# The RWKV-7 recurrence inside a deep fp32 block stack: each step taken straight from the state instead of from a map formed per chunk and head

## The chip, the cores and the metric

One Trainium2 chip, one core of it. The metric is the device time of one execution in microseconds; lower is better. The program is built ahead of time: for each engine (TensorE, VectorE, ScalarE, GpSimd, and SyncE, which starts the DMA transfers) the order of its instructions is fixed when it is built, each engine takes its own list in that order, and an instruction that has to wait holds back everything behind it on that engine. In the profile the engines are called PE, DVE, ACT, POOL and SP.

## The reference

A stack of transformer-like blocks in fp32 on 512 tokens: projections, several kinds of attention, gated feed-forward layers. The part that matters is one mixer (the "even" one) whose second half of the heads is an RWKV-7 recurrence: 8 heads of width 64, a 64x64 state S for each head, run once forwards and once backwards over the tokens. First the context tokens are scanned, then the latent ones start from the context's last state:

```python
def step(S, inp):
    r, w, k, v, kk, a = inp
    S = (S * w[:, :, None, :]
         - jnp.einsum('bhvk,bhk->bhv', S, kk)[..., None] * (kk * a)[:, :, None, :]
         + v[..., None] * k[:, :, None, :])
    return S, jnp.einsum('bhvk,bhk->bhv', S, r)
...
S_cf, y_cf = wkv7_scan(S0, dir_inputs(f_ctx, 0), reverse=False)
S_cb, y_cb = wkv7_scan(S0, dir_inputs(f_ctx, 1), reverse=True)
_, y_lf = wkv7_scan(S_cf, dir_inputs(f_lat, 0), reverse=False)
_, y_lb = wkv7_scan(S_cb, dir_inputs(f_lat, 1), reverse=True)
o_lat = rwkv7_readout(y_lf + y_lb, f_lat, r_k, gn_w, gn_b)
```

Each token decays the state (w), removes what the state holds along kk, adds the product of v and k, and reads the state with r. The other half of that mixer's heads is ordinary attention, which does not depend on the recurrence.

## The kernel before, in words

The scan is done in chunks of 64 tokens. The 512 tokens are four tiles of 128 tokens, two chunks each; a tile in one direction is a *unit*, so there are eight units, and eight *steps*, each of which takes one chunk in the forward direction and one in the backward direction (d = 0, 1) further. Both directions share every instruction: the forward chunk lies on one half of the 128 partitions, the backward chunk on the other.

For each unit, before its steps:

- *front* and *back* (`rwkv_in`) make the decayed vectors. `ar` holds, per head pair, the decay on a diagonal, the read vectors and the removal vectors; `g` holds, per head and chunk, what the chunk's tokens add to the state (columns 0 to 63), the token-by-token products that outputs read (64 to 127) and those that the removal reads (128 to 191).
- Within a chunk the removals depend on one another through a unit lower triangular 64x64 matrix per head and chunk, which has to be inverted. *solve* (`rwkv_solve`) inverts its 16x16 diagonal pieces for two units at once by 28 small DVE operations on two tiles `dl` and `dt`, loaded by a DMA from a DRAM buffer `dq` and stored by a DMA to a DRAM buffer `dy`.
- `rwkv_maps` loads those pieces as `x` (L1603), and extends them to the whole inverse by two rounds of `product` and `update` (all four go through `each`, L1609). Then it forms, per chunk and head, the chunk's *map*: `am` holds the removal vectors transposed (L1635) and the values times the removal products (the third kind of product at L1609, `m<-lw,g`); the inverse is applied to it (L1649); the result is copied into `lw`, beside the values `v` that were loaded there (L1588); and `lw` times `g` (L1663), plus `ar`, is written over `g` as `z`.

`z` is one matrix per chunk and head which, multiplied with the state, gives the next state and the chunk's outputs. For that the state tiles `si` hold, beside each head's 64x64 state on one half of the partitions, an identity on the other half, written once at the start; the values pass through it. Two `si` tiles alternate.

`rwkv_step` then is two groups of 16 matmuls: the next state (L1681), copied out of PSUM by DVE for the even heads and ACT for the odd ones into the other `si` tile, and the outputs (L1690), written to `yac` by ACT for the first direction that reaches a tile and added to `yac` by DVE for the second.

What sets the order: `rwkv` runs four *blocks* p = 1 to 4. In each, `maps_of(p-1)` makes the maps of two units and takes two steps; after every `yield` of it one piece of the independent attention is issued (`fill`), then two pieces of `ahead_of(p)`, which prepares the next two units (back, solve, front), and two pieces of the gates and readouts of finished tiles. `ahead_of` has nothing left in the fourth block. The scheduler that builds the program takes the instructions in about this order and interleaves them on each engine by what is ready. After the fourth block comes `mixed`, the projection back to the residual, which needs the outputs of all steps; its weight loads start behind the last step.

PSUM has two buffers with the name `m` here, which all the products share, and one `y`, used by the steps.

## Time and profile before

| what | time |
|---|---|
| median of 3 runs | 2336.53 us |
| lowest and highest of them | 2333.61 and 2338.04 us |
| the profiled execution, its own time | 2338.83 us |
| the span of the profiled execution | 2337.0 us |

The span is the time from the first to the last instruction of the profiled execution; the views below all belong to that one execution. PE is busy for 2250.4 us of it. The recurrence, with the attention woven into it, lies between about 929 and 1173 us from the start of the span. A matmul in fp32 appears as two records in the trace, each with a time of its own; "busy" for PE counts the union of overlapping records, while the mean ns of a group is the length of one record, overlaps and all. The granted clock (PEclk) is a share of the full 2.4 GHz: 1.00 is that level all the time, 0.50 is 1.2 GHz all the time.

### The profile page before, as it was taken

The numbers are of one execution on the slowest core, as the hardware profiler recorded it, in microseconds if no ns is written. First come the engines' busy times: TensorE is split into PE (matmuls) and PEld (weight loads), VectorE is DVE, ScalarE is ACT, GpSimd is POOL, SyncE is SP. The second block draws the span as 40 slices with busy tenths as digits, with TensorE's granted clock in tenths as the row PEclk, the third lists the DMA queues.
The fourth block names the chain that finished last, engine by engine and source line by source line (L and its number), as shares of the span: only waits on it lengthen the run. The fifth ranks groups of instructions, "written<-read, shape, count | busy, mean of one in ns | idle before, by whom it ended". The sixth has DMA issues, their size and how long they took to land.

```text
span 2337.0 us, 35487 instructions
## 1 busy us (share of the span) xinstructions
PE 2250.4 (96%) x13714; PEld 1841.1 (79%) x13714; DVE 1563.4 (67%) x2993; ACT 1074.5 (46%) x1887; POOL 5.6 (0%) x10
## 2 busy tenths in 40 slices
PE   8999999999999998998889999999999999999998
PEld 6688788877787786776667778787778788768998
DVE  7867778766845768878588677437755334787555
ACT  6756666322224638765535222224422223476444
POOL 0000000000000000000000000000000000000000
PEclk9999999999999999999989999999999999999999
DMA  8556544554623535332354455323553222314553
GB/s 294 175 185 207 179 149 163 191 179 159 202 96 110 172 139 146 102 91 69 85 203 145 166 189 176 131 89 121 179 189 125 92 98 92 104 37 142 185 183 119
DMA packets 161944, 342.01 MB, mean 146 GB/s; under 512 B 48624, under 2 KB 76272, under 8 KB 161648
## 3 DMA queue, kind: packets, MB, share of 16 engines
q1 hardware_dynamic: 161056, 339.15, 43.8%
q8 instruction: 108, 1.77, 0.3%
q10 hardware_dynamic: 720, 0.60, 0.1%
q14 instruction: 60, 0.49, 0.1%
HBM read 321.86 MB, written 17.84 MB: 145 GB/s over the span
## 4 chain that ended last, share of the span: by engine, by line
PE 88%; DVE 6%; ACT 4%; DMA 2%; issue 1%; SPq 0%; DVEq 0%; ACTq 0%
PE mm L113 25%; PE mm L115 24%; PE mm L114 24%; PE m L1609 1%; PE tr L217 1%; PE m L1663 1%; DVE wlo L96 1%; PE po L1047 1%; PE wm L272 1%; PE wm L329 1%; PE gg L1540 1%; PE tr L1047 1%; ACT whi L95 1%; PE po L531 1%; PE y L1681 1%
## 5 line engine op out<-in xcount | busy, mean ns | idle before, releaser
L95 ACT CAST whi<-raw 128x1024 fp32r<-128x1024 f32 (+2 forms) x437 | 437.3, 1001 | 956.9 <-PE mm L114 587.4
L113 PE MATMUL mm<-xh,whi 128*128 128x512 f32 (+1 forms) x1912 | 679.8, 359 | 12.8 <-ACT xh L95 5.7
L115 PE MATMUL mm<-xh,wlo 128*128 128x512 f32 (+1 forms) x1912 | 679.2, 356 | 4.7 <-DVE wlo L96 4.3
L114 PE MATMUL mm<-xl,whi 128*128 128x512 f32 (+1 forms) x1912 | 679.1, 356 | 1.2 <-DVE xl L96 1.1
L96 DVE TENSOR_TENSOR wlo<-raw,whi 128x1024 fp32r<-128x1024 f32 (+2 forms) x437 | 507.9, 1164 | 249.5 <-ACT whi L95 243.1
L113 PEld LDWEIGHTS mm<-xh,whi 128*128 128x128 f32 x1912 | 363.4, 191 | 77.1 <-ACT whi L95 17.4
L115 PEld LDWEIGHTS mm<-xh,wlo 128*128 128x128 f32 x1912 | 363.9, 191 | 58.2 <-DVE wlo L96 8.4
L114 PEld LDWEIGHTS mm<-xl,whi 128*128 128x128 f32 x1912 | 364.3, 191 | 55.2 <-DVE xl L96 3.9
L115 PE MATMUL mm<-hh,wlo 128*128 128x512 f32 (+1 forms) x704 | 260.3, 370 | 0.0
L114 PE MATMUL mm<-hl,whi 128*128 128x512 f32 (+1 forms) x704 | 258.4, 367 | 0.1
L113 PE MATMUL mm<-hh,whi 128*128 128x512 f32 (+1 forms) x704 | 257.0, 366 | 0.0
L127 DVE SCALAR_TENSOR_TENSOR macc<-raw,modc,macc 128x1024 f32<-128x1024 f32 x189 | 234.9, 1280 | 0.8 <-DMA raw<-in_w_mod 0.3
L127 DVE SCALAR_TENSOR_TENSOR xres<-mm,mod,xres 128x256 f32<-128x256 f32 x216 | 96.6, 480 | 161.8 <-PE mm L115 161.4
L118 DVE TENSOR_TENSOR fg<-mm,fg 128x512 f32<-128x512 f32 (+1 forms) x84 | 52.4, 624 | 162.2 <-PE mm L115 162.1
L113 PEld LDWEIGHTS mm<-hh,whi 128*128 128x128 f32 x704 | 132.2, 188 | 27.6 <-ACT whi L95 2.5
L114 PEld LDWEIGHTS mm<-hl,whi 128*128 128x128 f32 x704 | 132.2, 188 | 26.1 <-DVE hl L96 0.7
L113 PE MATMUL mm<-whi,xh 128*128 128x512 f32 (+1 forms) x360 | 143.6, 404 | 8.9 <-ACT whi L95 8.4
L115 PEld LDWEIGHTS mm<-hh,wlo 128*128 128x128 f32 x704 | 132.5, 188 | 22.8
L114 PE MATMUL mm<-wlo,xh 128*128 128x512 f32 (+1 forms) x360 | 143.5, 399 | 2.8 <-DVE wlo L96 2.8
L115 PE MATMUL mm<-whi,xl 128*128 128x512 f32 (+1 forms) x360 | 141.9, 396 | 0.0
L113 PEld LDWEIGHTS mm<-whi,xh 128*128 128x128 f32 x360 | 68.7, 191 | 30.0 <-issue 9.2
L114 PEld LDWEIGHTS mm<-wlo,xh 128*128 128x128 f32 x360 | 69.0, 192 | 17.1 <-DVE wlo L96 5.2
(401 smaller groups left out, 2539.6 us busy)
## 6 DMA issues: line engine op xcount, KB each, us to landing
raw<-in_ffn_in SPq DMA_DIRECT2D x176, 512.0 KB, 3.5
raw<-in_w_mod SPq DMA_DIRECT2D x144, 512.0 KB, 4.5
raw<-in_ffn_out SPq DMA_DIRECT2D x64, 448.0 KB, 3.2
raw<-in_w_in_even SPq DMA_DIRECT2D x32, 512.0 KB, 4.9
raw<-in_w_in_odd SPq DMA_DIRECT2D x32, 512.0 KB, 4.1
raw<-in_ffn_out SPq DMA_DIRECT2D x32, 512.0 KB, 3.6
raw<-in_w_ple_gate SPq DMA_DIRECT2D x16, 512.0 KB, 3.7
raw<-in_even_r SPq DMA_DIRECT2D x15, 512.0 KB, 3.6
```

The source lines that it names most:

```text
L95: S.copy(out=hi, in_=src)
L96: V.tensor_tensor(out=lo, in0=src, in1=r32(hi), op=ALU.subtract)
L113: E.matmul(out=ps, lhsT=ah, rhs=bh, start=first, stop=False)
L114: E.matmul(out=ps, lhsT=ah, rhs=bl, start=False, stop=False)
L115: E.matmul(out=ps, lhsT=al, rhs=bh, start=False, stop=last)
L118: V.tensor_tensor(out=o, in0=a, in1=b, op=op)
L127: V.scalar_tensor_tensor(out=o, in0=a, scalar=s, in1=b, op0=op0, op1=op1)
L217: E.transpose(ps[:, j * 128:(j + 1) * 128], s, ident)
L272: E.matmul(out=ps[32 * j:32 * j + 32, hf * 256:hf * 256 + 256], lhsT=cz[:, 4 * g + j, 10 - 2 * c:42 - 2 * c], rhs=raw[:, j], start=c == 0 ...
L329: E.matmul(out=ps[32 * j:32 * j + 32], lhsT=mod_1[:, 2 - q:34 - q], rhs=acc[:, v, hf * 512:hf * 512 + 512], start=q == 0, stop=q == 2)
L531: E.matmul(out=po[:, 0:128], lhsT=pt[:, j * 128:(j + 1) * 128], rhs=vt[:, j, c], start=j == 0, stop=j == nk - 1)
L1047: E.matmul(out=po[half(a), 0:256], lhsT=vt[:, j], rhs=pt[:, j, 2 * a:2 * a + 2], start=j == 0, stop=j == nk - 1)
```

## The change

No map is formed. `rwkv_maps` becomes `rwkv_inverse`: the inverse is built as before, the values are loaded into a tile `uv` of their own (four buffers), and the product of the values with the removal products, which went to `am`, goes to a new tile `kv`. The transposes of the removal vectors, the application of the inverse to `am`, the tiles `lw`, and the 16 matmuls, 4 additions and 4 copies per unit that made `z` are gone. The state tiles no longer hold an identity.

Each step then has four stages instead of two. The removal vectors times the state (8 matmuls, L1640) are added to `kv` by DVE; the inverse is applied to the sum (16 matmuls, L1646), and the result is copied into the free halves of `uv` by DVE for one direction and by ACT for the other; the next state (L1657) sums, in PSUM, decay times state and `g` times `uv` (32 matmuls); the outputs (L1665) sum read vectors times state and `g` times `uv` (32 matmuls), in a PSUM buffer `m` instead of `y`. There is a `yield` after the addition and after the copies into `uv`, so a step has three slots instead of one, and a unit's inverse has five instead of seven: a block has 11 slots instead of 9. The last step makes no next state.

```diff
-            eye2 = C["eye2"]
-            C["lw"] = []
-            for n in range(2):
-                C["lw"].append([pk.tile([128, 4, 4, 64], F32, tag=f"lw{n}{ch}", name=nm("lw")) for ch in range(2)])
...
-                for par in range(2):
-                    hb = half(1 - par)
-                    for d in range(2):
-                        acopy(x[hb, d, par], eye2[hb].unsqueeze(1).to_broadcast([64, 4, 64]))
...
-                    for n in (0, 1) if p % 2 == 0 else (2, 3):
-                        yield from rwkv_step(n, tiles, z, si, yac)
+                def steps(p, kv):
+                    us = sorted(order[2 * p:2 * p + 2], key=lambda un: un["d"])
+                    for s in range(2):
+                        n = 2 * (p % 2) + s
+                        yield from rwkv_step(C, us, s, kv[s], si[n % 2], si[1 - n % 2] if p < 3 or s == 0 else None, yac, n < 2)
...
-    def rwkv_maps(C, D, un):
...
+    def rwkv_inverse(C, D, un, kv):
...
+        uv = un["uv"] = wk.tile([128, 2, 8, 64], F32, tag="uv", name=nm("uv"), bufs=4)
         for ch in range(2):
-            nc.sync.dma_start(out=lw[ch][half(1 - ch), :, 1:3],
-                              in_=D["v"][half(ch), t].rearrange("p (f a v) -> p f a v", f=4, a=2))
+            nc.sync.dma_start(out=uv[half(1 - ch), ch], in_=D["v"][half(ch), t].rearrange("p (h v) -> p h v", h=8))
...
         T = product(1)
-        am = w512("am", (128, 4, 4, 64))
...
+        ps = pst("m")
+        each(ps, lambda ch, h: g[half(1 - ch), h, ch, 128:192], lambda ch, h: uv[half(1 - ch), ch, h])
+        for ch in range(2):
+            acopy(kv[ch ^ d][half(ch)], v8(ps[half(ch)]))
+        yield
+        update(T)
+        un["x1"] = x1
+        yield
...
+    def rwkv_step(C, us, s, kv, s0, s1, yac, new):
+        at = [(d, un, s ^ d, half(s ^ d), slice(64 * (s ^ d), 64 * (s ^ d) + 64)) for d, un in enumerate(us)]
         ps = pst("m")
         for f in range(4):
+            for d, un, ch, cb, cc in at:
+                E.matmul(out=ps[cb, f * 128:(f + 1) * 128], lhsT=un["ar"][:, f, 2, cc], rhs=s0[:, d, :, f], start=True, stop=True)
+        tt(kv, kv, ps.rearrange("p (h t) -> p h t", h=8), ALU.add)
+        yield
         ps = pst("m")
+        for h in range(8):
+            for d, un, ch, cb, cc in at:
+                E.matmul(out=ps[cb, h * 64:(h + 1) * 64], lhsT=un["x1"][cb, h], rhs=kv[cb, h], start=True, stop=True)
+        for (d, un, ch, cb, cc), cp in zip(at, (vcopy, acopy)):
+            cp(un["uv"][cb, ch], ps[cb].rearrange("p (h t) -> p h t", h=8))
         yield
...
+        if s1 is not None:
+            ps = pst("y")
+            for d, un, ch, cb, cc in at:
                 for f in range(4):
+                    for i in range(2):
+                        for par in range(2):
+                            lh, rh = ((un["ar"][:, f, 0, cc], s0[:, d, par, f]), (un["g"][:, 2 * f + par, ch, 0:64], un["uv"][:, ch, 2 * f + par]))[i]
+                            E.matmul(out=ps[half(par), d * 256 + f * 64:d * 256 + f * 64 + 64], lhsT=lh, rhs=rh, start=i == 0, stop=i == 1)
+            for par, cp in ((0, vcopy), (1, acopy)):
+                cp(s1[half(par), :, par].rearrange("p d f v -> p d (f v)"), ps[half(par)].rearrange("p (d x) -> p d x", d=2))
+        ps = pst("m")
+        for h in range(8):
+            for i in range(2):
+                for d, un, ch, cb, cc in at:
+                    lh, rh = ((un["ar"][:, h // 2, 1, cc], s0[:, d, h % 2, h // 2]), (un["g"][:, h, ch, 64:128], un["uv"][:, ch, h]))[i]
+                    E.matmul(out=ps[cb, h * 64:(h + 1) * 64], lhsT=lh, rhs=rh, start=i == 0, stop=i == 1)
+        for d, un, ch, cb, cc in at:
+            y = yac[cb, un["t"] % 2]
+            if new:
+                acopy(y, ps[cb])
             else:
+                tt(y, y, ps[cb], ALU.add)
         yield
```

Outside the recurrence the order of the instructions on each engine stays as it was. Three places inside it follow, all of the second block. In these rows the numbers behind a name tell its buffers apart.

On PE before, at the first of the block's two steps: the end of the maps (L1663) and the next state (L1681), with attention (L1019, L1001) and the next unit's back stage (L1540) between them.

```order
L1019 MATMUL tr_10621<-ident_63,gp_10564 128x128 x2
L1663 MATMUL m_10488<-g_9377,lw_9086 128x128 x4
L1663 MATMUL m_10495<-g_9377,lw_9086 128x128 x4
L1681 MATMUL y_10525<-si_9089,g_9377 64x64
L1001 MATMUL sc_10840<-K_10830,qS_10832 128x512 x2
L1681 MATMUL y_10525<-si_9089,g_9377 64x64 x7
L1540 MATMUL gg_10662<-ar_10648,ak_10052 128x128
L1540 MATMUL gh_10663<-ar_10648,ak_10052 128x128
```

On PE after, from the removal of that step to its next state, in two pieces (the rows between are more of L1646 and the same attention).

```order
L1640 MATMUL m_10415<-si_9081,ar_9157 64x128
L1640 MATMUL m_10415<-si_9081,ar_9352 64x128
L1001 MATMUL sc_10425<-K_9122,qS_9892 128x256 x2
L1019 MATMUL tr_10433<-ident_63,gp_10369 128x128 x2
L1388 MATMUL fr_10761<-ro_9095,ro_9096 128x512
L1646 MATMUL m_10437<-kv_9917,x_2092_9923 64x64
L1646 MATMUL m_10437<-kv_9917,x_2095_9931 64x64
L1665 MATMUL m_10503<-si_9081,ar_9157 64x64
L1001 MATMUL sc_10456<-K_9122,qS_9892 128x256 x2
L1665 MATMUL m_10503<-si_9081,ar_9352 64x64
L1388 MATMUL fr_11129<-ro_9095,ro_9096 128x512
L1657 MATMUL y_10468<-uv_9919,g_9170 64x64 x2
```

The step's stages L1640, L1646, the first matmuls of L1665 (which need only the state) and L1657 now stand apart, with attention (L1001, L1019) and the gates' matmul (L1388) between them.

On DVE before, in the same block: the next units' solve (`dt`, `dl`) alternates with the additions that made the maps (`g<-m,ar`) and with the next unit's back stage (`ak`).

```order
L118 TENSOR_TENSOR ak_10052<-ak_10052,fe_10644 128x4x128
L118 TENSOR_TENSOR dt_10288<-dl_10270 128x54
L118 TENSOR_TENSOR g_9182<-m_10446,ar_9169 64x4x128
L118 TENSOR_TENSOR dl_10270<-dl_10270,dt_10288 128x6x9
L1005 RECIPROCAL s_10504<-s_10502 128x1
L118 TENSOR_TENSOR ak_10052<-ak_10052,fe_10644 128x4x2x64
L118 TENSOR_TENSOR dt_10291<-dl_10270 128x56
L118 TENSOR_TENSOR g_9182<-m_10453,ar_9169 64x4x128
L118 TENSOR_TENSOR dl_10270<-dl_10270,dt_10291 128x7x8
```

On DVE after, at the corresponding part of the solve.

```order
L118 TENSOR_TENSOR dl_10273<-dl_10273,dt_10294 128x7x8
L118 TENSOR_TENSOR yac<-yac,m_10503 64x512
L118 TENSOR_TENSOR dt_10297<-dl_10273 128x56
L118 TENSOR_TENSOR yac<-yac,m_10503 64x512
L118 TENSOR_TENSOR dl_10273<-dl_10273,dt_10297 128x8x7
L224 COPY gpt_10360<-tr_10539 128x2x128
L118 TENSOR_TENSOR dt_10300<-dl_10273 128x54
L118 TENSOR_TENSOR kv_9918<-kv_9918,m_10543 128x512
L118 TENSOR_TENSOR dl_10273<-dl_10273,dt_10300 128x9x6
```

The solve now alternates with the steps' own DVE work: additions into `yac` and `kv`, and an attention copy (`gpt`).

On SP before, around the store of that solve's result (`dy`): loads of `v` into `lw` (L1588) stand ahead of it.

```order
L1433 DMA oTd<-go_10443 128x2x128
L1389 DMA ro_9112<-lod 128x128 x2
L1588 DMA lw_9081<-vd 64x4x128
L1588 DMA lw_9082<-vd 64x4x128
L1588 DMA lw_9085<-vd 64x4x128
L1445 DMA K_10830<-kd 128x1024
L1447 DMA qS_10834<-qd 128x512
L1588 DMA lw_9086<-vd 64x4x128
L1582 DMA dy_7266<-dl_10270 64x16x16
L1582 DMA dy_7267<-dl_10270 64x16x16
```

On SP after, around the same store and the load of its result (`x`).

```order
L1500 DMA fe_10727<-fd 128x12x128
L1437 DMA K_10580<-kd 128x1024
L1439 DMA qS_10584<-qd 128x512
L1381 DMA ro_9096<-lod 128x128 x2
L1425 DMA oTd<-go_10558 128x2x128
L1574 DMA dy_7266<-dl_10273 64x16x16
L1574 DMA dy_7267<-dl_10273 64x16x16
L1596 DMA x_2213_10701<-dy_7266 64x8x64 x2
L1582 DMA uv_11520<-vd 64x512 x2
```

The loads into `lw` are gone; the load of `v`, now into `uv`, stands behind the load of `x`.

## Rows read from the trace of the kernel before

**Rows 1.** Page parts 1 and 4: busy us, share; chain by line.

```profile
PE 2250.4 (96%) x13714; PEld 1841.1 (79%) x13714; DVE 1563.4 (67%) x2993; ACT 1074.5 (46%) x1887; POOL 5.6 (0%) x10
...
PE mm L113 25%; PE mm L115 24%; PE mm L114 24%; PE m L1609 1%; PE tr L217 1%; PE m L1663 1%; DVE wlo L96 1%; PE po L1047 1%; PE wm L272 1%; PE wm L329 1%; PE gg L1540 1%; PE tr L1047 1%; ACT whi L95 1%; PE po L531 1%; PE y L1681 1%
```

**Rows 2.** Windows, four blocks, last steps: length, busy us, PEclk.

```profile
929.00:1000.50 71.50, 64.25 (x771) 50.21 (x771) 56.54 (x132) 52.27 (x128) 5.39 (x6) 0.91 0.45 115
...
1000.50:1062.00 61.50, 58.10 (x777) 46.84 (x778) 44.65 (x103) 38.48 (x95) 0.00 (x0) 0.92 0.32 83
...
1062.00:1126.50 64.50, 55.11 (x742) 43.36 (x737) 55.21 (x130) 35.04 (x63) 0.00 (x0) 0.97 0.35 92
...
1126.50:1173.00 46.50, 39.87 (x631) 32.77 (x630) 24.03 (x48) 22.30 (x48) 0.00 (x0) 0.91 0.20 54
...
1143.90:1174.20 30.30, 23.29 (x284) 19.52 (x280) 15.02 (x27) 15.97 (x32) 0.00 (x0) 0.83 0.12 33
```

**Rows 3.** PE groups, 929 to 1173: busy us, mean ns, idle before.

```profile
L1663 PE MATMUL m<-g,lw 128*128 128x128 f32 x256 | 35.4, 284 | 2.3 <-ACT lw L221 1.1 <-ACT g L221 1.1
...
L1609 PE MATMUL m<-x,g 64*64 64x64 f32 x512 | 21.6, 232 | 2.8 <-DVE s L124 2.1 <-ACT am L221 0.7
...
L1609 PE MATMUL m<-x,T 64*64 64x64 f32 x512 | 20.8, 223 | 0.3 <-DVE T L118 0.3
...
L1649 PE MATMUL m<-am,x 64*64 64x128 f32 x256 | 17.5, 275 | 1.4 <-ACT lw L221 1.1
...
L1681 PE MATMUL y<-si,g 128*64 128x64 f32 x256 | 14.8, 248 | 4.2 <-ACT g L221 1.7 <-DVE yac L118 1.6 <-ACT yac L221 0.6
...
L1690 PE MATMUL y<-si,g 128*64 128x64 f32 x256 | 11.5, 258 | 5.5 <-ACT si L221 5.5
...
L1609 PE MATMUL m<-lw,g 64*64 64x64 f32 x256 | 9.9, 222 | 1.1 <-ACT am L221 0.9 <-issue 0.2
...
L1635 PE MATMUL m<-ident,ar 128*128 128x128 f32 x32 | 5.2, 287 | 0.0
```

**Rows 4.** Waits, 929 to 1173: us, times, longest.

```profile
PEld m L1609 <- issue: 6.3, 20, 2.2
```

**Rows 5.** Timeline, PE, second block: start us, us, what.

```profile
1061.11 1.15 PE L1690 MATMUL y<-si,g 128*64 128x64 f32 x32 [0.81 <-ACT si L221]
```

**Rows 6.** DVE and ACT groups, 929 to 1173.

```profile
L118 DVE TENSOR_TENSOR g<-m,ar 64x512 f32<-64x512 f32 x32 | 22.0, 687 | 6.6 <-PE m L1663 5.7
...
L221 ACT COPY lw<-m 64x512 f32<-64x512 f32 x32 | 18.5, 579 | 3.0 <-PE m L1649 2.6
...
L221 ACT COPY g<-m 64x512 f32<-64x512 f32 x32 | 18.5, 578 | 9.1 <-DVE g L118 8.4
```

**Rows 7.** Timeline, last two steps: start us, us, what [idle before].

```profile
1162.62 0.68 DVE L224 COPY si<-y 64x512 f32<-64x512 f32 x1 [1.93 <-PE y L1681]
...
1163.33 0.58 ACT L221 COPY si<-y 64x512 f32<-64x512 f32 x1 [1.48 <-DVE si L224]
...
1163.96 1.83 PE L1690 MATMUL y<-si,g 128*64 128x64 f32 x32 [1.38 <-ACT si L221]
...
1167.37 1.98 PE L1681 MATMUL y<-si,g 128*64 128x64 f32 x32 [1.58 <-DVE yac L118]
...
1170.74 1.97 PE L1690 MATMUL y<-si,g 128*64 128x64 f32 x32 [1.39 <-ACT si L221]
...
1172.75 0.33 SPq L100 DMA_DIRECT2D raw<-in_even_out  x1
```

**Rows 8.** SP queue: waits 929 to 1173; timeline of one load.

```profile
SPq L1588 <- PE m L1663: 26.3, 8, 8.9
...
1057.72 1.25 SPq L1603 DMA_DIRECT2D x<-dy  x2
```

**Rows 9.** Timeline, DVE, second block: solve, first and last.

```profile
1032.50 0.17 DVE L118 TENSOR_TENSOR dt<-dl 128x14 f32<-128x14 f32 x1
...
1048.08 0.18 DVE L118 TENSOR_TENSOR dl<-dl,dt 128x14 f32<-128x14 f32 x1
```

More of the change, by code (lines that the diff above doesn't have):

```diff
@@ L1289, in rwkv @@
                 side = iter(())
-                def steps(p):
-                    tiles = ((2, 3), (0, 1))[p // 2]
-                    z = {(un["d"], un["t"]): un["z"] for un in order[4 * (p // 2):2 * p + 2]}
-                    for n in (0, 1) if p % 2 == 0 else (2, 3):
-                        yield from rwkv_step(n, tiles, z, si, yac)
+                def steps(p, kv):
[3 more added lines that the diff above has]
+                        yield from rwkv_step(C, us, s, kv[s], si[n % 2], si[1 - n % 2] if p < 3 or s == 0 else None, yac, n < 2)
                 def ahead_of(p):
@@ L1308, in maps_of @@
                 def maps_of(p):
-                    for _ in itertools.zip_longest(*(rwkv_maps(C, D, order[u]) for u in (2 * p, 2 * p + 1))):
+                    kv = [C["wk"].tile([128, 8, 64], F32, tag=f"kv{i}", name=nm("kv")) for i in range(2)]
+                    for _ in itertools.zip_longest(*(rwkv_inverse(C, D, order[u], kv) for u in (2 * p, 2 * p + 1))):
                         yield
@@ L1314, in maps_of @@
                         yield from read
-                    yield from steps(p)
+                    yield from steps(p, kv)
                 for p in range(1, 5):
@@ L1639, in rwkv_maps @@
-        acopy(am[:, :, 1:3], ps.rearrange("p (f a t) -> p f a t", f=4, a=2))
-        yield
-        update(T)
-        yield
-        for i in range(2):
-            ps = pst("m")
-            for j in range(4):
-                h = 4 * i + j
-                for ch in range(2):
-                    cb = half(ch)
-                    E.matmul(out=ps[cb, j * 128:(j + 1) * 128], lhsT=x1[cb, h], rhs=am[cb, h // 2, 2 * (h % 2):2 * (h % 2) + 2],
-                             start=True, stop=True)
-            for ch in range(2):
-                acopy(lw[ch][half(ch), 2 * i:2 * i + 2], ps[half(ch)].rearrange("p (f a t) -> p f a t", f=2, a=4))
@@ L1654, in rwkv_maps @@
-        yield
-        z = g.rearrange("p (f a) c t -> p c a f t", a=2)[:, :, :, :, 0:128]
-        for ch in range(2):
-            for par in range(2):
-                ps = pst("m")
-                pz = ps.rearrange("p (f t) -> p f t", f=4)
-                hb, vb = half(par), half(1 - par)
-                for f in range(4):
-                    h = 2 * f + par
-                    E.matmul(out=ps[:, f * 128:(f + 1) * 128], lhsT=lw[ch].rearrange("p f a t -> p f (a t)")[:, f, par * 128:(par + 1) * 128],
-                             rhs=g[:, h, ch, 0:128], start=True, stop=True)
-                tt(z[hb, ch, par].rearrange("p f (a t) -> p f a t", a=2), pz[hb].rearrange("p f (a t) -> p f a t", a=2),
-                   ar[hb, :, 0:2, ch * 64:ch * 64 + 64], ALU.add)
-                acopy(z[vb, ch, par], pz[vb])
@@ L1668, in rwkv_maps @@
-        un["z"] = z
-        yield
-    def rwkv_step(n, tiles, z, si, yac):
-        s0, s1 = si[n % 2], si[1 - n % 2]
-        where = []
-        for d in range(2):
-            c = n if d == 0 else 3 - n
-            where.append((d, tiles[c // 2], c % 2))
-        ps = pst("y")
-        for d, t, ch in where:
-            for f in range(4):
-                for par in range(2):
-                    E.matmul(out=ps[half(par), d * 256 + f * 64:d * 256 + f * 64 + 64], lhsT=z[d, t][:, ch, par, f, 0:64],
-                             rhs=s0[:, d, par, f], start=True, stop=True)
-        for par, cp in ((0, vcopy), (1, acopy)):
-            cp(s1[half(par), :, par].rearrange("p d f v -> p d (f v)"), ps[half(par)].rearrange("p (d x) -> p d x", d=2))
-        ps = pst("y")
-        for f in range(4):
-            for par in range(2):
-                for d, t, ch in where:
-                    h = 2 * f + par
-                    E.matmul(out=ps[half(ch), h * 64:(h + 1) * 64], lhsT=z[d, t][:, ch, par, f, 64:128], rhs=s0[:, d, par, f], start=True, stop=True)
-        for d, t, ch in where:
-            cb = half(ch)
-            if n < 2:
-                acopy(yac[cb, t % 2], ps[cb])
```

10 lines of the change are left out of this document (2 added, 8 removed).

## The prediction

> **What bounds the kernel now.** I read the page first. PE is busy for 96% of the span, and the chain that ended last is mostly matmuls of the projections (L113 to L115); the lines of the recurrence have about 1% of it each [rows 1]. So the whole kernel is bound by PE, and whatever shortens PE's list where nothing else is late shortens the span; but the change touches one stage, and that has to be read by itself. The windows come second: 929 to 1173 us, cut at the end of each block's last step [rows 2]. PE is busy for 64.25, 58.10, 55.11 and 39.87 us of 71.5, 61.5, 64.5 and 46.5, which is 217.3 of 244 us; DVE for 180.4, ACT for 148.1 (the sums of those four rows). The stage is PE's, with 26.7 us in which PE idles; no other engine is near it, though over a few us DVE can be. The third view, PE's groups in the stage, says what that work is and where it idles [rows 3]: the two costliest groups are L1663, which forms the maps (35.4 us), and the products L1609, which stay.
>
> The last 30 us are of another kind: PE is busy for 23.3 of 30.3 us, at a granted clock of 0.83, and no attention is left to fill it [rows 2]. The timeline there shows a bare chain [rows 7]: DVE copies half of the state (0.68), ACT the other half only after it (0.58), and each of the last two output groups has waited 1.4 us for ACT. The first weight load of the projection that follows (`raw<-in_even_out`) is issued at 1172.75, some 0.04 us after the last output group ends (1170.74 + 1.97). There a microsecond of the steps is a microsecond of the span.
>
> **The change part by part: PE.** Gone are the map products 35.4, the application of the inverse 17.5, the steps' two groups 14.8 and 11.5, and the transposes 5.2 [rows 3]: 84.4 us. Added are, in records (two for each fp32 matmul), over eight steps:
>
> - Removal times state, 8 matmuls of 128 columns a step: 128 records. The nearest row is L1649, also 128 columns: 17.5 / 256 = 68 ns each. 8.7 us.
> - The inverse, 16 of 64x64 a step: 256 records. The three L1609 groups are the same shape: (21.6 + 20.8 + 9.9) / 1280 = 41 ns. 10.5 us.
> - Next state, 32 a step for seven steps (the last has none), and outputs, 32 a step for eight: 448 + 512 = 960 records of 64 columns. At best they stream as the group at 1061.11 does, 1.15 us for 32 or 36 ns [rows 5]; the two groups that they replace took (14.8 + 11.5) / 512 = 51 ns on average, the half-rate stretches included. I take 42, nearer to the streaming row, since the new groups are twice as long and wait as a whole: 40.3 us, with 34.5 and 49 as ends.
>
> That is 59.5 us (53.7 to 68.2). PE's work goes down by **25 us** (16 to 31). Nothing in it is off the path except what only fills an idle gap; in the first three blocks PE's list has attention behind each group, so what goes out moves that attention forward.
>
> **Waits.** The idle time of PE just before the removed groups and before the product from `lw` is 2.3 + 1.4 + 1.1 + 4.2 + 5.5 = 14.5 us [rows 3]; these go. New are three hand-overs a step: the addition to `kv` on DVE (0.69 by the `g<-m,ar` addition, [rows 6]), the copies into `uv` (0.68 on DVE and 0.58 on ACT, one after the other as the `si` copies are, so 1.3; [rows 7]), and the same 1.3 for the next state. In the last block nothing covers the first two: 2 x (0.7 + 1.3) = 4.0, and 0.6 for semaphores. The third is covered by the step's own outputs (64 records, 2.3 us at 36 ns) before the next step's removal. In the other six steps the order puts attention between the stages; I take 1.2 us a step there, the size of one uncovered copy, 7 in all. New waits 11.6, net **-3**. If attention covers all of them only the last block's 4.6 stay, net -10; if nothing does, 8 x 3.3 = 26.4 come, net +12.
>
> **The other engines.** DVE loses the 32 additions (22.0 us), ACT 32 copies into `lw` and 32 into `g` (18.5 each) and the copies of `am`; what comes (eight additions and eight copies on DVE at 0.69, eight copies and sixteen of `kv` on ACT at 0.58) is about 11 and 14 us [rows 6]. Off the path, so no term, except that ACT's copies into `g` had stood 8.4 us behind DVE's additions. The eight identity copies and four memsets at the start lie in a stretch with ACT at 52 of 71 us [rows 2] and are costed at nothing. On SP, the loads of `v` into `lw` had waited 26.3 us for L1663, eight times [rows 8], and held the loads behind them; those waits go. The solve is 28 small DVE operations between 1032.50 and 1048.08 [rows 9], held up by being interleaved with additions; its result is loaded at 1057.72 [rows 8], 9.6 us after it was done.
>
> **Sum.** -25 - 3 = -28 us on the profiled execution, 2338.8 to 2310.8. That execution was 2.3 us over the median, so against the median 2336.5 - 28 = **2308.5 us**. As a check from the other side, the last block: its 30.3 us hold 14 us or so of removed work and waits and get back two steps of the new kind. Two steps at full rate are (16 + 32 + 128) x 2 records less the 64 of the missing next state, 288 records at 40 ns or 11.5 us, plus 4.6 of waits, 16 to 17; at the lower clock (1.9 against 1.15 us for the same 32 records, [rows 5, 7]) some 22. The block gives 8 to 13 us, and the other three have to give 5 to 7 each.
>
> One thing in the trace speaks against this. PE's weight loads at L1609 had 20 waits that no event explains, 6.3 us in all, 0.32 each, the longest 2.2 [rows 4], where 64x64 work begins. The Trainium skill has a rule for it, in "TensorEngine Tiling (Array Packing)", section Key Properties: a change of the tiling mode drains TensorE. The trace agrees in kind; no row isolates it. A step now goes into and out of 128x64, 64x64 and again 128x64 tiles with 128x128 attention between, six changes against about four before; two more for eight steps at 0.32 us are an estimated 5 us, so by that rule the sum would be -23, without it -28.
>
> **Rivals.**
>
> *Only the last block gains.* Blocks 1 to 3 are held by the preparation of the next units: load, decay products, solve, store, load. For it: solve and load take from 1032.50 to 1057.72 [rows 8, 9], most of the second block's latter half. Against it: PE is busy for 58.1 of the 61.5 us there [rows 2], so that chain was covered. The last block gives its 11, the rest nothing: 2325.5.
>
> *More than the work.* With SP's queue free, the load of the solve's result comes up to 8.9 us earlier [rows 8], and PE, which ran at 0.92 of the clock there [rows 2], has less at the lower level (0.08 x 61.5 is some 5 us of clock, of which I count 3). -28 - 9 - 3 = -40: 2296.5. Against it stands the same 58.1 of 61.5.
>
> *The lower clock takes it back.* Steps with waits between small groups are where PE is at 1.2 GHz: 1.83 to 1.97 us for what takes 1.15 [rows 5, 7]. At that ratio, 1.65, two thirds of the 59.5 us of new work at the lower level cost 26 us more: -28 + 26, no change, 2334.5. For it: 0.83 in the last window. Against it: 0.91 to 0.97 where there is attention.
>
> *Slower.* Each of the three hand-overs waits not for its 0.7 us operation but for DVE's list: the solve's 28 operations and the attention's now stand between the `kv`, `uv` and `si` operations in blocks 1 to 3, and PE, which takes its list in order, cannot go past a waiting stage. If a step idles 7 us (2.3 at each hand-over), eight cost 56: 56 - 14.5 - 25 = +16, 2352.5. It decides from about 5 us a step (39.5 / 8). For it: the solve's 15.6 us for 28 operations of 0.17 to 0.18 [rows 9] show how crowded that list is; against it: DVE is busy for 73% of the second block [rows 2] and loses 22 us of additions.
>
> **How the numbers follow.** My forecast 0.53 (its own range 2296 to 2323: -41 from the lower ends of work and waits, down to -14 with either at its bad end); only the last block 0.16; more than the work 0.16; the lower clock 0.06; slower 0.09. Under 0.2%, some 4.7 us, a measurement of this kernel cannot tell from no change. The first three are faster, 0.85; the fourth is the same, 0.06; the last slower, 0.09. The range 2292 to 2330 takes in the first three with the bounds of their terms and leaves out the other two and a little at the low end.
>
> **What would show it.** PE's busy time in the stage: 192 us against 217 if the sum of the work is right; L1657 and L1665 together 34 to 49 us. PE's idle time before L1646, L1657 and L1640: 12 us in all, half of it in the last two steps; 40 or more would mean the slower rival, and it would name DVE's `kv` or `uv` as the releaser. From the block's last attention to the issue of `raw<-in_even_out`: 16 to 22 us where it was 30.3. If blocks 1 to 3 keep 71.5, 61.5 and 64.5 us while PE idles more, it is the first rival. If the load of `x` comes within 2 us of the solve's end and the second block is shorter by more than 10 us, it is the second. The forecast is wrong if the new small groups run near 1.65 times their streaming time in all blocks, or if PE's list, with less in it, only waits longer for the same loads.

## The result, and the profile of the kernel after

The median went from 2337.28 us (2333.61 to 2340.43, four runs) to **2307.52 us** (2305.60 to 2315.90, four runs); the ratio is 0.988, its 95% interval 0.9855 to 0.9904. That is 29.8 us between the medians, where 28 had been forecast (2308.5 us, 2292 to 2330).

The profiled execution took 2308.39 us, with a span of 2306.6. The page, parts 1 and 4:

```profile
PE 2226.5 (97%) x14002; PEld 1820.1 (79%) x14002; DVE 1550.7 (67%) x2976; ACT 1038.9 (45%) x1822; POOL 2.0 (0%) x6
...
PE mm L113 25%; PE mm L115 25%; PE mm L114 25%; PE m L1602 2%; PE tr L217 1%; PE wm L272 1%; PE po L1047 1%; PE wm L329 1%; DVE wlo L96 1%; PE gg L1532 1%; PE m L1665 1%; PE tr L1047 1%; PE po L531 1%; ACT whi L95 0%; DMA x<-dy 0%
```

The chain is the projections' as before [rows 1]. PE is busy for 23.9 us less, though it has 288 more records. The stage still begins at 929 us and now ends, with the first `raw<-in_even_out`, at 1141.49 instead of 1172.75: 31.3 us earlier, so the whole gain is in it. Its four blocks, each cut within 0.3 us of the end of its last output group, and the stage (length, busy us of PE, PEld, DVE, ACT, POOL, granted clock, DMA):

```profile
929.00:990.90 61.90, 58.80 (x875) 46.28 (x876) 49.88 (x122) 36.59 (x90) 1.84 (x2) 0.89 0.47 124
990.90:1041.90 51.00, 48.78 (x834) 38.36 (x833) 41.92 (x101) 30.60 (x81) 0.00 (x0) 1.00 0.42 99
1041.90:1105.20 63.30, 54.94 (x851) 42.44 (x851) 56.48 (x136) 32.62 (x72) 0.00 (x0) 0.95 0.35 89
1105.20:1141.49 36.29, 29.20 (x642) 24.44 (x642) 20.01 (x39) 13.15 (x29) 0.00 (x0) 0.95 0.35 96
929.00:1141.49 212.49, 191.71 (x3198) 151.52 (x3198) 168.29 (x396) 112.95 (x270) 1.84 (x2) 0.94 0.40 103
```

The stage of the kernel before, cut in the same way at its load:

```profile
929.00:1172.75 243.75, 217.33 (x2910) 173.18 (x2910) 180.19 (x411) 148.10 (x333) 5.39 (x6) 0.93 0.34 89
```

PE's busy time falls by 25.6 us and its idle time by 5.6 (26.4 to 20.8). The cuts of [rows 2] were rounded: the kernel before ended its blocks' last output groups at 1003.3, 1062.3, 1123.2 and 1172.7, so the blocks went from 74.3, 59.0, 61.0 and 49.5 us to 61.9, 51.0, 63.3 and 36.3. The third got longer: with eleven slots instead of nine the attention moves forward, the third block holds more of it and the last block less. PE's time for it (L1001, L1019, L1047) goes from 11.7 to 17.2 us in the third block and from 14.0 to 7.0 in the last, so 7 of the 13.2 us by which the last block got shorter are work that moved.

The four new groups, one row each in the order L1640, L1646, L1657, L1665 (PE and weight loads busy, over the stage):

```profile
929.00:1141.49 212.49, 8.70 (x128) 6.82 (x128) 0.94 0.40 103
...
929.00:1141.49 212.49, 9.93 (x256) 8.42 (x256) 0.94 0.40 103
...
929.00:1141.49 212.49, 18.79 (x448) 16.15 (x448) 0.94 0.40 103
...
929.00:1141.49 212.49, 21.07 (x512) 18.41 (x512) 0.94 0.40 103
```

And the idle time before them, from the groups of lines (after the second bar). These rows count both halves of an alternating pair in full, which is why the first numbers of L1657 and L1665 add up to more than the windows above:

```profile
L1665 PE MATMUL m<-uv,g 128*64 128x64 f32 x256 | 17.4, 229 | 0.8 <-DVE uv L224 0.5 <-ACT uv L221 0.3
...
L1657 PE MATMUL y<-uv,g 128*64 128x64 f32 x224 | 15.9, 233 | 2.9 <-ACT uv L221 1.9 <-DVE uv L224 1.0
L1646 PE MATMUL m<-kv,x 64*64 64x64 f32 x256 | 9.9, 222 | 1.8 <-DVE kv L118 1.8
...
L1640 PE MATMUL m<-si,ar 128*64 128x128 f32 x128 | 8.7, 278 | 0.6 <-DVE x L118 0.6
```

The last two steps, which answer to [rows 7]:

```profile
1124.87 0.59 PE L1047 MATMUL tr<-gpt,vv 128*64 128x256 f32 x2
...
1125.89 1.15 PE L1646 MATMUL m<-kv,x 64*64 64x64 f32 x32 [0.43 <-DVE kv L118]
...
1127.08 0.68 DVE L224 COPY uv<-m 64x512 f32<-64x512 f32 x1 [1.25 <-PE m L1646]
...
1129.18 0.62 ACT L95 CAST xh<-orel 128x512 fp32r<-128x512 f32 x1 [3.31 <-DMA oTd<-go]
1129.82 0.58 ACT L221 COPY uv<-m 64x512 f32<-64x512 f32 x1
...
1130.45 0.48 PE L1657 MATMUL y<-uv,g 128*64 128x64 f32 x4 [1.48 <-ACT uv L221]
...
1134.57 1.04 PE L1640 MATMUL m<-si,ar 128*64 128x128 f32 x16
1136.20 0.69 DVE L118 TENSOR_TENSOR kv<-kv,m 128x512 f32<-128x512 f32 x1
...
1136.94 1.15 PE L1646 MATMUL m<-kv,x 64*64 64x64 f32 x32 [1.33 <-DVE kv L118]
...
1141.49 0.42 SPq L100 DMA_DIRECT2D raw<-in_even_out  x1
```

The bare chain is there: addition, inverse, copies. ACT's copy at 1129.82 starts 2.06 us after DVE's has ended, since a cast that had waited 3.31 us for a DMA stood ahead of it in ACT's list; PE then waited 1.48 us for that copy.

### The profile page after: what moved, and what is told of

Same layout as the page of the kernel before. It is cut to its first block, busy times and chain, and to the rows that moved or that the text cites. A ratio compares the mean times of both kernels' runs of the same rounds, so it can differ in the third digit from the quotient of the medians.

```text
span 2306.6 us, 35981 instructions
## 1 busy us (share of the span) xinstructions
PE 2226.5 (97%) x14002; PEld 1820.1 (79%) x14002; DVE 1550.7 (67%) x2976; ACT 1038.9 (45%) x1822; POOL 2.0 (0%) x6
## 4 chain that ended last, share of the span: by engine, by line
PE 89%; DVE 5%; ACT 3%; DMA 2%; issue 1%; SPq 0%; DVEq 0%; ACTq 0%
PE mm L113 25%; PE mm L115 25%; PE mm L114 25%; PE m L1602 2%; PE tr L217 1%; PE wm L272 1%; PE po L1047 1%; PE wm L329 1%; DVE wlo L96 1%; PE gg L1532 1%; PE m L1665 1%; PE tr L1047 1%; PE po L531 1%; ACT whi L95 0%; DMA x<-dy 0%
## 5 line engine op out<-in xcount | busy, mean ns | idle before, releaser
L115 PEld LDWEIGHTS mm<-hh,wlo 128*128 128x128 f32 x704 | 132.4, 188 | 22.9
L113 PEld LDWEIGHTS mm<-whi,xh 128*128 128x128 f32 x360 | 68.6, 191 | 29.7 <-issue 9.3
L114 PEld LDWEIGHTS mm<-wlo,xh 128*128 128x128 f32 x360 | 69.0, 192 | 16.9 <-DVE wlo L96 4.9
```

The source lines that it names most:

```text
L113: E.matmul(out=ps, lhsT=ah, rhs=bh, start=first, stop=False)
L114: E.matmul(out=ps, lhsT=ah, rhs=bl, start=False, stop=False)
L115: E.matmul(out=ps, lhsT=al, rhs=bh, start=False, stop=last)
```

## The experiments

Several theories stood at first. *PE's list*: the stage takes what PE has to do, so the gain is the matmuls that went and a few waits. Against it: only the last block gains, the evictions of the maps (ACT and DVE) were the cost, SP's queue was, or the attention's new place. All times are medians; "against before" is against the kernel before on the same chip, the changed kernel being at -29.8. The ratio and its interval are estimated from all runs, so the ratio need not be that of the two medians.

To read the traces side by side, each stage (929 us to the first `raw<-in_even_out`) is split into three parts: over stretches of 2 us, PE's busy time multiplied by the granted clock, added up, is **work**, what PE would be busy for at the full clock; the rest of the busy time is what the lower **clock** cost; and the stage less the busy time is **idle**.

| kernel | against before | ratio, 95% interval | stage | work | clock | idle |
|---|---|---|---|---|---|---|
| before | 0 | | 243.8 | 202.9 | 14.4 | 26.4 |
| after | -29.8 | 0.9880, 0.9855 to 0.9904 | 212.5 | 181.4 | 10.3 | 20.8 |
| map_matmuls_back | -15.5 | 0.9936, 0.9911 to 0.9961 | 230.2 | 207.1 | 9.3 | 13.8 |
| evictions_back | -2.7 | 0.9996, 0.9975 to 1.0016 | 245.8 | 179.3 | 29.7 | 36.8 |
| values_in_two_buffers | -21.7 | 0.9911, 0.9896 to 0.9926 | 221.9 | 179.0 | 19.3 | 23.6 |
| before_with_more_attention_early | 0.0 | 1.0008, 0.9995 to 1.0020 | 239.7 | 206.6 | 5.2 | 27.9 |
| before_queue_freed | -11.6 | 0.9953, 0.9938 to 0.9968 | 229.9 | 200.9 | 5.6 | 23.3 |
| maps_and_evictions_back | +1.4 | 1.0002, 0.9993 to 1.0012 | 244.5 | 210.8 | 10.1 | 23.6 |
| state_halves_first | -30.2 | 0.9867, 0.9852 to 0.9882 | 211.7 | 180.6 | 10.2 | 20.8 |
| attention_kept_for_the_end | -32.8 | 0.9863, 0.9847 to 0.9880 | 206.0 | 177.9 | 5.1 | 22.9 |
| attention_store_off_queue | -30.7 | 0.9862, 0.9847 to 0.9877 | 210.1 | 179.8 | 11.0 | 19.3 |
| one_more_operation_in_each_step | -26.1 | 0.9878, 0.9858 to 0.9899 | 214.8 | 179.9 | 12.9 | 22.1 |
| before_attention_loads_off_queue | -1.6 | 0.9986, 0.9976 to 0.9996 | 235.3 | 201.8 | 5.0 | 28.5 |
| three_together | -27.7 | 0.9878, 0.9862 to 0.9893 | 215.0 | 175.4 | 12.5 | 27.2 |

The three parts come from one execution of each kernel. The eight kernels with the changed kernel's matmuls differ in work by 6.0 us (175.4 to 181.4), the four with the matmuls of before by 5.7. The clock's part is 5.0 to 5.6 in three kernels made from the one before, which has 14.4 itself, and two of the three are within 1.6 us of it in time. So a difference of 6 us in work, or of 10 in the clock's part, says nothing by itself.

**The maps' matmuls back** (`map_matmuls_back`).

```diff
         update(T)
         un["x1"] = x1
+        for ch in range(2):
+            for par in range(2):
+                ps = pst("m")
+                for f in range(4):
+                    E.matmul(out=ps[:, f * 128:(f + 1) * 128], lhsT=g[:, 2 * f + par, ch, 0:128], rhs=g[:, 2 * f + par, ch, 0:128], start=True, stop=True)
```

> The changed kernel with the maps' 16 matmuls per unit (128x128 by 128 columns, 256 records in all) issued again into PSUM at the end of each unit's inverse, from g; nothing reads them, so no copy, addition or wait comes back. Theory 'PE's list': the stage is bound by what PE has to do, so the span grows by nearly all of their 35 us, 30 to 36 us over the changed kernel. Rival 'only the last block': blocks 1 to 3 are held by the preparation of the next units, so only the last block's quarter shows, 9 us and at most 15.

Measured: 14.3 us over the changed kernel, less than half of what PE's list would make of it and within the rival's bound. But the place is not the rival's: the blocks' last output groups end at 996.33, 1053.34, 1119.10 and 1159.17 us here, so the four blocks are 5.7, 5.9, 2.3 and 3.8 us longer than in the changed kernel. The stage of this run, to be held against the changed kernel's above:

```profile
929.00:1159.20 230.20, 216.43 (x3454) 179.80 (x3454) 169.24 (x398) 113.14 (x270) 1.84 (x2) 0.95 0.36 97
```

PE is busy for 24.7 us more and the stage is 17.7 longer: 7 us of the new work lies in what had been idle time. PE's list is not the whole of the stage; 1:1 is too dear a price for PE's work here.

**The evictions back** (`evictions_back`), read from the products' PSUM tiles a second time:

```diff
+        def more(ps):
+            tt(ev[0]..., v8(ps[half(0)]), C["tmask"]..., ALU.add)
+            acopy(ev[1], ps[half(1)])
+            acopy(ev[1], ps[half(1)])
...
             tt(x1, x1, v8(ps), ALU.add)
+            more(ps)
```

> The changed kernel with 64 ACT copies and 32 DVE additions of 64x512 out of PSUM added (8 and 4 per unit, read a second time from the products' PSUM tiles and stored to a scratch tile), about what the maps' evictions took (37 and 22 us); no matmul is added. Theory 'PE's list': ACT and DVE are off the path, 0 to 6 us over the changed kernel. Rival 'evictions': the 29 us came from ACT and DVE being relieved, so at least 12 us come back.

Measured: 27.1 us over the changed kernel, with no matmul added. It overstates its case, since the readers here stand inside the inverse and hold one of the two `m` buffers between its products; that is why the next pair was run.

**Maps and evictions back** (`maps_and_evictions_back`), at the place where the maps were formed:

```diff
+                    E.matmul(out=ps[:, f * 128:(f + 1) * 128], lhsT=g[...], rhs=g[...], start=True, stop=True)
...
+                tt(sc[0], pz[half(par)], un["ar"][half(par), :, 0:2, ch * 64:ch * 64 + 64], ALU.add)
+                acopy(sc[1], ps[half(1 - par)])
```

> The changed kernel with the maps' matmuls issued again (as in the run that put them back, 16 us) and each of their PSUM tiles read as the maps were, by a 64x512 addition on DVE and a 64x512 copy on ACT into a scratch tile (32 of each), nobody waiting for these. Theory 'PE's list': evictions beside PE's work cost little, 0 to 5 us over the run with the matmuls alone, 16 to 21 us over the changed kernel. Rival 'evictions': the copies and additions cost by themselves what the other run showed, so 28 us or more over the changed kernel.

Measured: 31.2 us over the changed kernel and 16.9 over the run with the matmuls alone. Evictions put back in this way were on the path. Where they sit (waits of this run: engine, line waited for, us, times, longest):

```profile
PE m L1656 <- DVE kv L118: 3.8, 3, 1.3
...
PE m L1637 <- ACT ev L221: 3.4, 6, 1.1
...
PE m L1650 <- ACT ev L221: 2.1, 2, 1.1
```

PE waits for an eviction to give back an `m` buffer (`ev`; L1637 the maps, L1650 the step's removal), and for DVE's addition, which now stands behind more in DVE's list (L1656 is the inverse in the step). Idle time is 9.8 us more than with the matmuls alone. They are not quite the evictions that went: all of them write one scratch tile, whose halves DVE and ACT take in turn, and ACT's copies stood 14.5 us behind DVE's additions, where those into `g` had stood 8.4 [rows 6]; and the 32 copies into `lw` were not put back.

**The values in two buffers** (`values_in_two_buffers`).

```diff
-        uv = un["uv"] = wk.tile([128, 2, 8, 64], F32, tag="uv", name=nm("uv"), bufs=4)
+        uv = un["uv"] = wk.tile([128, 2, 8, 64], F32, tag="uv", name=nm("uv"), bufs=2)
```

> The changed kernel with the tile uv in two buffers instead of four, so that the load of the values stands on the SP queue until the steps of the block before have read uv, as it stood behind the maps before. Theory 'PE's list': SP's queue is not on the path, within 3 us of the changed kernel. Rival 'more than the work' (the queue's waits were part of the loss): 9 us or more over it.

Measured: 8.1 us over the changed kernel, near the rival's number. The four runs (2315.97 to 2318.64) lie above the changed kernel's four, the lowest by little (2315.90 is the highest there). But the loads hardly stood on the queue: SP's waits at them add up to 1.3 us in this run. They were issued later (the last at 1111.1 instead of 1052.7), among the loads of `x`, and 8.2 of the 9.4 us by which the stage is longer lie in the last block. What in this cost the 8.1 us stays open; it is no second proof that the queue's waits were. The clock's part rises by 9.0 us, idle by 2.8.

**The queue freed in the kernel before** (`before_queue_freed`), meant as the same from the other side:

```diff
+        vs = wk.tile([128, 512], F32, tag="vs", name=nm("vs"), bufs=2)
         for ch in range(2):
-            nc.sync.dma_start(out=lw[ch][half(1 - ch), :, 1:3], in_=...)
+            nc.sync.dma_start(out=vs[half(1 - ch)], in_=D["v"][half(ch), t])
+        for ch in range(2):
+            nc.gpsimd.tensor_copy(out=lw[ch][half(1 - ch), :, 1:3], in_=vs[half(1 - ch)]...)
```

> The kernel before with the values loaded into a small tile of two buffers, whose loads wait for nothing, and copied by GpSimd from there into lw (16 copies of 64x256); everything else is as before, so SP's queue no longer stands behind the maps. Theory 'PE's list': the gain came from PE's work (25.6 us less busy in the stage) and its idle time, so this stays within 3 us of the kernel before. Rival 'more than the work': the queue's waits were a part of the loss, as the 10 us of the run with two buffers suggest, so 6 to 12 us under the kernel before.

Measured: 11.6 us under the kernel before, so what this edit frees was on the path. It did not free the queue altogether; the loads into `vs` still wait on SP, 19.4 us where those into `lw` had waited 26.3 [rows 8]:

```profile
SPq L1589 <- POOL lw L1591: 19.4, 3, 13.4
```

The second block's last load of `x` starts at 1053.89 instead of 1057.72 [rows 8], and its last output group ends at 1054.27 instead of 1062.26. The second block's end in the kernel before (windows, columns as above):

```profile
1022.00:1032.00 10.00, 9.86 (x126) 7.39 (x125) 5.42 (x13) 7.19 (x18) 0.00 (x0) 1.00 0.35 77
1032.00:1042.00 10.00, 9.88 (x94) 8.12 (x91) 9.53 (x33) 8.31 (x21) 0.00 (x0) 1.00 0.32 90
1042.00:1052.00 10.00, 8.00 (x60) 6.36 (x59) 7.95 (x22) 6.62 (x21) 0.00 (x0) 0.81 0.44 120
1052.00:1062.00 10.00, 9.19 (x114) 6.35 (x114) 5.58 (x11) 4.46 (x10) 0.00 (x0) 0.68 0.28 66
```

and with the queue freed:

```profile
1022.00:1032.00 10.00, 9.75 (x125) 7.22 (x124) 5.25 (x16) 7.92 (x18) 0.00 (x0) 1.00 0.45 109
1032.00:1042.00 10.00, 9.20 (x75) 7.72 (x76) 9.75 (x27) 7.70 (x21) 1.86 (x3) 1.00 0.16 47
1042.00:1052.00 10.00, 8.76 (x128) 7.02 (x128) 8.98 (x25) 6.94 (x21) 0.61 (x1) 1.00 0.42 120
1052.00:1062.00 10.00, 9.52 (x146) 7.39 (x144) 8.81 (x17) 4.60 (x11) 0.00 (x0) 1.00 0.39 91
```

PE is busy for 9 us of 10 in the last row either way; but in the kernel before it had dropped to 8.0 in the row ahead of it, the granted clock fell to 0.81 and 0.68, and the same busy time does a third less. So the "same 58.1 of 61.5" that the prediction held against this rival was partly PE at the lower clock. That the queue cost its 11.6 us through the clock is not shown, though: in the next two runs the clock is 1.00 in the last two of these rows as well, with PE busy for 16.3 and 17.5 of the 20 us (17.2 before), and neither kernel gains as much.

**Only the attention's loads off the queue** (`before_attention_loads_off_queue`), to tell whose lateness it was.

```diff
-                        nc.sync.dma_start(out=r32(K), in_=D["k"][:, 2 * kv:2 * kv + 2])
+                        nc.gpsimd.dma_start(out=r32(K), in_=D["k"][:, 2 * kv:2 * kv + 2])
...
-                    nc.sync.dma_start(out=r32(qS), in_=D["q"][:, q, 4 * kv:4 * kv + 4])
+                    nc.gpsimd.dma_start(out=r32(qS), in_=D["q"][:, q, 4 * kv:4 * kv + 4])
```

> The kernel before with only the attention's loads of K and q started by GpSimd instead of SP; the loads into lw stay where they were and hold the recurrence's own loads (dy, x, fe) as before. If the queue's harm was that attention came late and left PE with gaps and the lower clock: 6 to 12 us under the kernel before, as with the queue freed. If it was the recurrence's own loads: within 3 us of the kernel before.

Measured: 1.6 us under the kernel before, the recurrence's side. The clock's part of the profiled execution, one of the faster ones (2333.74 us), is as low as with the queue freed (5.0), without the 11.6 us of time. Which load carries these stays open.

**The kernel before with the attention given out as after** (`before_with_more_attention_early`).

```diff
-                        fill(FP)
+                        fill(2 if p < 4 and i in (1, 3) else FP)
```

> The kernel before with the attention given out as the changed kernel does it: 11 pieces instead of 9 in each of blocks 1 to 3, and what is left in the fourth. Theory 'PE's list': attention only changes its place, within 5 us of the kernel before. Rival 'redistribution': a good part of the gain comes from the two slots more per block, 10 us or more under the kernel before.

Measured: 0.0, with the clock's part down to 5.2. The two slots more, by themselves, are not where the gain is.

**State halves first** (`state_halves_first`):

```diff
...
-        for h in range(8):
-            for i in range(2):
+        for i in range(2):
+            for h in range(8):
...
```

> The changed kernel with the next state's and the outputs' matmuls in another order: first the 16 that need only the state, then the 16 that need uv, so that the copies into uv run beside 16 matmuls. Theory 'waits are small': PE idles 3.7 us before these groups (2.9 and 0.8), so 2 to 4 us less. Rival: each hand-over stands behind DVE's list rather than behind its own copy, and the order of the matmuls changes nothing, within 1 us or above.

Measured: 0.4 us under the changed kernel, inside the interval. (The sums of eight heads are then one group each in PSUM, opened by the first matmul and closed by the last.) Its rows say why:

```profile
L1640 PE MATMUL m<-si,ar 128*64 128x128 f32 x128 | 10.0, 281 | 2.7 <-ACT si L221 2.7
L1646 PE MATMUL m<-kv,x 64*64 64x64 f32 x256 | 9.8, 222 | 2.7 <-DVE kv L118 2.7
...
L1657 PE MATMUL y<-uv,g 128*64 128x64 f32 x224 | 9.3, 226 | 0.3 <-ACT uv L221 0.3
```

The wait before L1657 is gone (2.9 to 0.3), as expected; the step's next hand-over has taken it up: 2.7 instead of 0.6 us before the next removal, for ACT's `si`. Before the four groups together PE idles for 5.7 us instead of 6.1.

**One more operation in each step** (`one_more_operation_in_each_step`).

```diff
         tt(kv, kv, ps.rearrange("p (h t) -> p h t", h=8), ALU.add)
+        vcopy(k2 := C["wk"].tile([128, 8, 64], F32, tag="k2", name=nm("k2")), kv)
+        kv = k2
```

> The changed kernel with one more DVE copy (128x512, some 0.69 us) between the addition to kv and the inverse of each step, eight in all. Theory 'waits are small': bare in the last block's two steps, mostly covered in the other six, 1 to 3 us over the changed kernel. Rival 'slower' (each hand-over waits for its turn in DVE's list): 1.7 us a step or more, 12 us and over.

Measured: 3.7 us over the changed kernel, with intervals that overlap. It excludes 12, and so the rival "slower"; it does not tell 1 from 6. The copy was shorter than expected, 0.42 us and not 0.69:

```profile
L224 DVE COPY k<-kv 128x512 f32<-128x512 f32 x8 | 3.3, 416 | 0.0
```

So 3.7 us is about the length of all eight, and no sign that six of them were covered.

**What is left?** Three edits of the changed kernel: the first is `attention_kept_for_the_end`, the second `attention_store_off_queue`, and both with the third are `three_together`.

```diff
-                        fill(FP)
+                        fill(0 if p < 4 and i in (1, 3) else FP)
...
-            nc.sync.dma_start(out=D["o"][:, 2 * kv:2 * kv + 2, q * 128:(q + 1) * 128], in_=o)
+            nc.scalar.dma_start(out=D["o"][:, 2 * kv:2 * kv + 2, q * 128:(q + 1) * 128], in_=o)
...
-        ps = pst("m")
+        pu = pst("m"), pst("y")
...
-                E.matmul(out=ps[cb, h * 64:(h + 1) * 64], lhsT=un["x1"][cb, h], rhs=kv[cb, h], start=True, stop=True)
+                E.matmul(out=pu[d][cb, h * 64:(h + 1) * 64], lhsT=un["x1"][cb, h], rhs=kv[cb, h], start=True, stop=True)
```

> The changed kernel with two of the attention's pieces left out of each of blocks 1 to 3, so that the last block's steps have attention beside them as far as it lasts. Theory 'waits are small': the last block's idle time (7.1 us) is covered and the first blocks lose cover that they hardly need, 2 to 6 us less. Rival: only the place of the attention changes, and blocks 1 to 3 idle more by what the last one gains, within 2 us.

> The changed kernel with the attention's output stores (oTd<-go, which stood on SP's queue for 35.8 us until ACT had made go) started by ACT itself behind its copy. Theory 'SP's queue is on the path' (two-buffer run +10, before with the queue freed -12): the loads behind them come earlier, 3 to 8 us under the changed kernel. Theory 'PE's list': within 2 us.

> The changed kernel with the attention kept for the last block, its stores started by ACT, and the two copies into uv read from two PSUM banks (the second is y), so that DVE and ACT copy at the same time. If queue and last block are what is left: 5 to 12 us under the changed kernel, 2296 to 2303. If they overlap or the gaps only move: within 3 us of the run with the attention kept, 2302 to 2308.

Measured: 3.0 and 0.9 us under the changed kernel, and 2.1 over it. Each interval overlaps the changed kernel's, so none is shown to be faster. Taking SP's 35.8 us of standing for that store off its queue bought nothing that these runs can show: a long wait on a queue need not be on the path.

## Why the prediction was right in size, and which of its steps were not

**The terms.** PE's new work: 8.7, 10.5 and 40.3 us were forecast for L1640, L1646 and the pair L1657/L1665; measured 8.70, 9.93 and 18.79 + 21.07 = 39.86. PE's busy time in the stage: 192 forecast, 191.7 measured. Waits: -3 forecast, idle time fell by 5.6. The new hand-overs idle PE for 0.6 + 1.8 + 2.9 + 0.8 = 6.1 us, where 11.6 were put down; the last two steps have 4.6 of these, as forecast (0.43 and 1.33 before the inverse, 2.8 before what reads `uv`), the other six 1.5 instead of 7. As a budget of PE's time the sum came out, 28 against 29.8.

**The causes.** A budget is not a list of causes, and here the experiments part from the prediction. Through the runs one can go from the kernel before to the one after in four steps:

| step | time, us | work | clock | idle |
|---|---|---|---|---|
| SP's queue freed (in part) | -11.6 | -2.0 | -8.8 | -3.1 |
| new steps for old; transposes, L1649, `lw` gone | +13.0 | +9.9 | +4.5 | +0.3 |
| the evictions of the maps gone | -16.9 | -3.7 | -0.8 | -9.8 |
| the matmuls of the maps gone | -14.3 | -25.7 | +1.0 | +7.0 |
| all | -29.8 | -21.5 | -4.1 | -5.6 |

(Each row is the difference of two rows of the table of runs; the first column in time, the others in the profiled stages. Taken in another order the steps would have other prices. By the intervals above, the times are uncertain by 3.5, 4, 6 and 8 us from the first row to the fourth; the parts to the right have the spread named under the table of runs.)

- "Off the path, so no term", of the additions and copies, was wrong: put back, they cost 16.9 us. In that run they held PSUM buffers and DVE's and ACT's lists, and PE waited for both. A part was in the sum under another name: of the 14.5 us of waits that go, 5.9 were PE's for ACT's copies `lw`, `g` and `am` [rows 3]. The prediction had also named the 8.4 us that ACT's copies stood behind DVE's additions [rows 6] and drew nothing from it.
- The queue's waits got a price only in the rival "more than the work", where 0.16 lay on it. That the queue had a price is shown in the kernel before (11.6 us); the run with two buffers after does not show it again. The rival's own sign did not appear: the changed kernel loads `x` at 1043.21 and 1047.15 us, 4 and 8 us after the solve's end at 1039.07 and not within 2, and the second block is 8.0 us shorter, not more than 10. Nor did its number, -40. And the 9.6 us between solve and load were misread: half of the result had been loaded at 1052.00, and what stood right ahead of the load at 1057.72 was the attention's store, not a load into `lw`:

```profile
1052.00 1.27 SPq L1603 DMA_DIRECT2D x<-dy  x2
1057.25 0.38 SPq L1433 DMA_DIRECT2D oTd<-go  x1
```

- PE's work was priced at 1:1. The maps' matmuls cost less than they take: 14.3 us of time (17.7 of stage in the profiled execution) for 24.7 of busy time; the rest had filled idle time. Also, the durations came from rows with the lower clock in them: in the two executions, 4.1 of the 25.6 us of busy time are clock, not work.
- The new steps' price in PE's time is right: 59.5 - (17.5 + 14.8 + 11.5 + 5.2) = 10.5 us forecast, 58.5 - 49.0 = 9.5 by PE's rows. In the table this step costs 13.0 us of time.

So the size came out partly by luck, by errors of opposite sign: a term counted in full that was worth a half to three quarters, and two that were left out or counted in part, the queue and the evictions.

**The places.** The last block gave 13.2 us (8 to 13 forecast), about 7 of them by the attention that moved out of it, which the forecast had not counted. Blocks 1 to 3 gave 18.1 together (15 to 21 forecast), but as 12.4, 8.0 and -2.3, not 5 to 7 each. "Only the last block gains" is refuted by that, and by the maps' matmuls put back, of which the last block carries 3.8 us of 17.7. The prediction also said that no attention is left in the last 30 us; the kernel before still had some:

```profile
1158.22 0.65 PE L1047 MATMUL tr<-gpt,vv 128*64 128x256 f32 x2
...
1159.89 0.86 PE L1047 MATMUL tr<-gpt,vv 128*64 128x256 f32 x5
...
1160.58 0.38 PE L1047 MATMUL tr<-gpt,vv 128*64 128x256 f32 x1
```

and the bare end that was to shrink from 30.3 us was 11.8 to begin with (1160.58 + 0.38 to 1172.75); after it is 16.0 (1124.87 + 0.59 to 1141.49).

**The other rivals.** "The lower clock takes it back": the clock's part did not rise in the profiled executions (14.4 before, 10.3 after), and the new groups L1657 and L1665 took 39.86 us, 1.16 times their streaming time of 34.5 and not 1.65; in the run with the evictions back the clock's part was 29.7, so the mechanism exists. "Slower": excluded by the result, since the new hand-overs idle PE for 6.1 us and not 56, and by the extra operation. The rule that a change of the tiling mode drains TensorE (the Trainium skill, "TensorEngine Tiling (Array Packing)", section Key Properties), from which the prediction estimated 5 us more, is not borne out in size. Unexplained waits of the weight loads after, for the 64-wide groups:

```profile
PEld m L1602 <- issue: 4.3, 19, 0.5
...
PEld y L1657 <- issue: 1.4, 7, 0.4
PEld m L1665 <- issue: 1.3, 3, 0.8
...
PEld m L1646 <- issue: 0.5, 3, 0.2
```

That is 7.5 us. The kernel before had 6.3 at L1609 [rows 4] and, at its steps,

```profile
PEld y L1681 <- issue: 3.8, 5, 1.7
```

so these waits got shorter in all, not longer.

## What to carry to other kernels

A sum of busy and idle time on the bound engine can come out right while its causes are wrong: put the removed parts back one kind at a time (matmuls, evictions, queue waits) before believing it. An eviction that holds one of two PSUM buffers can be on the bound engine's path even when its own engine idles much of the time, as ACT did here (busy for 148.1 of 243.8 us). And busy time at a lower granted clock looks like work: read the two together before concluding that a wait was covered, and in more than one kernel's trace before calling the clock a cause.

## What the runs showed of the hardware that was not expected

- Idle time of PE and time lost to the 1.2 GHz level do not move together. With the values in two buffers idle time rose by 2.8 us and the time lost to the lower level by 9.0, with the evictions inside the inverse by 16.0 and 19.4; but with the maps' evictions added to their matmuls by 9.8 and 0.8, and with the attention's loads off the queue idle time rose by 2.1 while the other fell by 9.4.
- Two copies out of one PSUM tile, on different halves of the partitions, are one after the other here: ACT's copy waits for DVE's (6.2 us in the changed kernel's stage). Read from two PSUM tiles they overlap:

```profile
1131.55 0.69 DVE L224 COPY uv<-m 64x512 f32<-64x512 f32 x1
1131.89 0.56 ACT L221 COPY uv<-y 64x512 f32<-64x512 f32 x1
```

That was run only together with two other edits (`three_together`), and the three together were not faster.
